# How two DMA rings share the first two loads of a gated SiLU: by partitions instead of by columns

## The chip, the cores and the metric

The kernel runs on one core of a Trainium2 chip. The metric is the device time of one execution in microseconds (us); the kernel before takes 471.64 us, the median of three runs (471.42 to 471.78). Two engines of the core issue the transfers: SyncE (SP in the profile) and ScalarE (ACT). Each has a ring, that is a queue of transfers, on each of the same 16 DMA engines; the profile calls SyncE's ring q1 and ScalarE's q10. A transfer is cut into packets, here one for each partition that it touches, and ends with a small completion mark on each DMA engine.

## The reference

The input has 32 x 512 = 16384 rows of 2048 float32 values. The first half of a row goes through SiLU and is multiplied by the second half:

```python
x1, x2 = x[..., :half_dim], x[..., half_dim:]
silu_x1 = x1 * (1 / (1 + np.exp(-x1)))
return silu_x1 * x2
```

So 134.22 MB are read from HBM and 67.11 MB are written.

## The kernel before

The rows are cut into 16 tiles of 1024 rows. Partition p of a tile holds K = 8 consecutive rows, 64 KB that are contiguous in HBM. Input tiles `xt` and output tiles `ot` are double buffered (`in_pool` and `out_pool`, two buffers each).

The order of the work is written out by hand in the loop over tiles. `load(0)` and `load(1)` are issued first. For each tile `silu` (ScalarE) writes silu of the first halves to `ot`, `mul` (VectorE) multiplies `ot` by the second halves in place, the result is stored by a transfer on ScalarE's ring, and `load(i + 2)` is issued on SyncE's ring. That load reuses the buffer of tile i, so it waits until `mul` of tile i has ended; the store waits for the same. `silu` of tile i waits for the tile's load, and for the store of tile i - 2 that used the same `ot` buffer. A middle tile is one `silu` and one `mul` over all 8 rows; tile 0 is done in four pieces of two rows (`KC_FIRST`), and the last tile in pieces of 2, 2 and 4 rows (`LAST`), each stored by SyncE as soon as it is done. `settle_all_but` makes SyncE see all earlier transfers land before those last ones.

All loads after the first two are one transfer of 8 MB on SyncE's ring. The first two are shared between the rings by `SHARED`: the dictionary holds the row (of the 8 in each partition) at which the tile is cut. Of tile 0, SyncE loads rows 0 to 3 of each partition and ScalarE rows 4 to 7; of tile 1, SyncE loads six rows and ScalarE two. Both transfers of a tile touch all 128 partitions. Line 54 issues every transfer, line 76 is the silu, line 83 the multiplication.

Of the kernel before, what the change touches and what calls it, by code (L numbers as in the profile page):

```python
# [1 line left out]

# [4 lines left out]


@with_exitstack
def kernel(  # L10
    ctx: ExitStack,
    tc: tile.TileContext,
    x: bass.AP,
    out: bass.AP,
):


    nc = tc.nc
    P = nc.NUM_PARTITIONS

    x_flat = x.flatten_outer_dims()
    out_flat = out.flatten_outer_dims()
    num_rows, in_cols = x_flat.shape
    half = in_cols // 2
    dt = x_flat.dtype

    K = 8
    KC_FIRST = 2
    LAST = (2, 2, 4)
    SHARED = {0: K // 2, 1: 3 * K // 4}  # L30
    PLAN = [K] * (num_rows // (P * K))

    in_pool = ctx.enter_context(tc.tile_pool(name="in_pool", bufs=2))
    out_pool = ctx.enter_context(tc.tile_pool(name="out_pool", bufs=2))

    plan = []
    row = 0
    for k in PLAN:
        plan.append((row, k))
        row += P * k  # L40
    assert row == num_rows
    n_tiles = len(plan)

    def view(flat, i):
        row0, k = plan[i]
        return flat[row0:row0 + P * k].rearrange("(p k) d -> p k d", k=k)

    ctx.enter_context(tc.manual_schedule())

    loaded = {}  # L50
    sent = []

    def move(queue, out, in_):
        sent.append(queue.dma_start(out=out, in_=in_).ins)  # L54

    def settle_all_but(n):
        rest = nc.sync.nop(nofuse=True)
        for ins in sent[:-n]:
            tc.add_manual_dep(
                rest.ins,  # L60
                ins.name,
                mybir.DependencyInfo(mybir.DependencyClass.Sync, mybir.DependencyReason.DATA),
                reason="sync sees each earlier transfer land before the last ones",
            )

    def load(i):
        xt = in_pool.tile([P, K, in_cols], dt, name="xt")
        xv = view(x_flat, i)
        cut = SHARED.get(i, K)
        move(nc.sync, xt[:, :cut], xv[:, :cut])  # L70
        if cut < K:
            move(nc.scalar, xt[:, cut:], xv[:, cut:])
        loaded[i] = xt

    def silu(ot, xt, c, ce):
        nc.scalar.activation(  # L76
            out=ot[:, c:ce, :],
            in_=xt[:, c:ce, :half],
            func=mybir.ActivationFunctionType.Silu,
        )  # L80

    def mul(ot, xt, c, ce):
        nc.vector.tensor_mul(  # L83
            out=ot[:, c:ce, :],
            in0=ot[:, c:ce, :],
            in1=xt[:, c:ce, half:],
        )

    load(0)
    load(1)  # L90
    for i in range(n_tiles):
        xt = loaded.pop(i)
        ov = view(out_flat, i)
        ot = out_pool.tile([P, K, half], dt, name="ot")
        if i < n_tiles - 1:
            kc = KC_FIRST if i == 0 else K
            for c in range(0, K, kc):
                silu(ot, xt, c, c + kc)
                mul(ot, xt, c, c + kc)
            move(nc.scalar, ov, ot)  # L100
            if i + 2 < n_tiles:
                load(i + 2)
            continue
        c = 0
        for kc in LAST:
            silu(ot, xt, c, c + kc)
            mul(ot, xt, c, c + kc)
            move(nc.sync, ov[:, c:c + kc], ot[:, c:c + kc])
            c += kc
        settle_all_but(len(LAST))  # L110


# [1 line left out]
_INS = ['x']  # L114
_OUTS = [((32, 512, 1024), 'float32')]


# [23 lines left out]
```

## Time and profile before

| what | value |
|---|---|
| median of three runs | 471.64 us |
| the profiled execution | 471.66 us, span 469.7 us |
| VectorE busy | 139.5 us (30%), 21 instructions |
| ScalarE busy | 114.2 us (24%), 22 instructions |
| one silu, one multiplication of a whole tile | 7.03 us, 8.69 us |
| HBM read and written | 134.22 MB and 67.11 MB, 429 GB/s over the span |
| time of the DMA packets | q1 65.3%, q10 34.2% of 16 engines' span |

A span is the time from the first to the last instruction in the profile. The shares of the rings say how long their packets kept the 16 DMA engines busy. The chain that ended last goes back from the last instruction: at each step to what released it. Times from issue to landing include the time that a transfer waits in its ring behind earlier ones.

### The profile page before, as it was taken

How to read it: one execution, taken by the hardware profiler on the slowest of the kernel's cores; microseconds unless marked ns; L12 is line 12 of the kernel's file. 1: busy time of each engine (PE TensorE's matmuls, PEld its weight loads, DVE VectorE, ACT ScalarE, POOL GpSimd, SP SyncE). 2: the span in 40 equal slices, each digit the busy share in tenths (PEclk: the TensorE clock that was granted, in tenths of full speed). 3: DMA queues.
4: the chain of work that ended last, by engine and by line, in shares of the span. 5: the costliest groups of instructions: out<-in, count | busy, mean ns of one | idle time of the engine just before them, and what ended most of it. 6: DMA issues, size and time to landing. Idle time of an engine off the chain costs nothing.

```text
span 469.7 us, 187 instructions
## 1 busy us (share of the span) xinstructions
DVE 139.5 (30%) x21; ACT 114.2 (24%) x22; POOL 0.2 (0%) x4
## 2 busy tenths in 40 slices
DVE  0070702407034070330704307042070520605142
ACT  1054105032050410504105050050501405014060
POOL 0000000000000000000000000000000000000000
DMA  8999999999999999999999999999999999999998
GB/s 357 424 447 424 402 444 455 441 402 435 413 491 402 410 438 491 402 402 447 474 419 402 447 430 463 402 435 413 491 402 407 441 491 402 402 447 474 419 402 357
DMA packets 5184, 201.33 MB, mean 429 GB/s; under 512 B 576, under 2 KB 576, under 8 KB 576
## 3 DMA queue, kind: packets, MB, share of 16 engines
q1 hardware_dynamic: 2736, 132.12, 65.3%
q10 hardware_dynamic: 2448, 69.21, 34.2%
HBM read 134.22 MB, written 67.11 MB: 429 GB/s over the span
## 4 chain that ended last, share of the span: by engine, by line
DMA 72%; DVE 14%; ACT 12%; ACTq 0%; issue 0%
DMA out_dram<-ot 63%; DVE ot L83 14%; ACT ot L76 12%; DMA xt<-in_x_dram 9%; ACTq L136 0%; ACTq L54 0%
## 5 line engine op out<-in xcount | busy, mean ns | idle before, releaser
L83 DVE TENSOR_TENSOR ot<-ot,xt 128x8192 f32<-128x8192 f32 (+2 forms) x21 | 139.5, 6659 | 321.8 <-ACT ot L76 321.8
L76 ACT ACTIVATE ot<-xt 128x8192 f32<-128x8192 f32 (+2 forms) x21 | 112.9, 5400 | 341.0 <-DMA out_dram<-ot 309.0
L76 ACT ACT_TABLE_LOAD x1 | 1.3, 1283 | 1.6 <-PEq L125 1.6
L125 POOL MEMSET const-bfloat16-1.0<- 128x1 bf16 x1 | 0.1, 101 | 0.0
L125 POOL MEMSET const-uint8-127<- 128x1 uint8 x1 | 0.1, 101 | 0.0
L125 POOL MEMSET const-float32-0.0<- 128x1 f32 x1 | 0.1, 98 | 0.2 <-issue 0.2
L125 POOL MEMSET const-float32-1.0<- 128x1 f32 x1 | 0.1, 98 | 0.0
## 6 DMA issues: line engine op xcount, KB each, us to landing
out_dram<-ot ACTq DMA_DIRECT2D x15, 4096.0 KB, 42.2
xt<-in_x_dram SPq DMA_DIRECT2D x1, 6144.0 KB, 40.9
xt<-in_x_dram ACTq DMA_DIRECT2D x1, 4096.0 KB, 22.1
xt<-in_x_dram SPq DMA_DIRECT2D x1, 4096.0 KB, 21.9
xt<-in_x_dram ACTq DMA_DIRECT2D x1, 2048.0 KB, 41.1
out_dram<-ot SPq DMA_DIRECT2D x2, 1024.0 KB, 7.8
out_dram<-ot SPq DMA_DIRECT2D x1, 2048.0 KB, 7.5
xt<-in_x_dram SPq DMA_DIRECT2D x14, 42.1
```

Of the source, the lines that this page charges most:

```text
L76: nc.scalar.activation(out=ot[:, c:ce, :], in_=xt[:, c:ce, :half], func=mybir.ActivationFunctionType.Silu,)
L83: nc.vector.tensor_mul(out=ot[:, c:ce, :], in0=ot[:, c:ce, :], in1=xt[:, c:ce, half:],)
L125: nc = _bacc.Bacc("TRN2", target_bir_lowering=False, num_devices=1)
```

## The change

`SHARED` is replaced by `SPLIT_LOADS`, which names for tiles 0 and 1 the partitions and the rows that each ring loads. Tile 0: SyncE loads the 64 even partitions, ScalarE the 64 odd ones, each with all 8 rows (64 KB). Tile 1: ScalarE loads the odd partitions in one transfer, SyncE the even ones in four: partitions 2, 6, 10, ... (32 of them), partitions 4, 12, 20, ... (16), and partitions 0, 8, 16, ... (16) twice, once for rows 0 to 3 and once for rows 4 to 7. For each of 16 DMA engines that is 2 + 1 + 1 + 1 packets on SyncE's ring and 4 on ScalarE's, if the partitions are spread evenly over the engines. All other loads and all stores stay as they are.

A tile of one column is added: VectorE sets it to zero, and ScalarE runs silu on it, after the first loads are issued and before tile 0.

```diff
-    SHARED = {0: K // 2, 1: 3 * K // 4}
+    EVERY = slice(None)
+    WHOLE = slice(0, K)
+    SPLIT_LOADS = {
+        0: ([(slice(0, None, 2), WHOLE)], [(slice(1, None, 2), WHOLE)]),
+        1: (
+            [
+                (slice(2, None, 4), WHOLE),
+                (slice(4, None, 8), WHOLE),
+                (slice(0, None, 8), slice(0, K // 2)),
+                (slice(0, None, 8), slice(K // 2, K)),
+            ],
+            [(slice(1, None, 2), WHOLE)],
+        ),
+    }
...
     def load(i):
         xt = in_pool.tile([P, K, in_cols], dt, name="xt")
         xv = view(x_flat, i)
-        cut = SHARED.get(i, K)
-        move(nc.sync, xt[:, :cut], xv[:, :cut])
-        if cut < K:
-            move(nc.scalar, xt[:, cut:], xv[:, cut:])
+        on_sync, on_scalar = SPLIT_LOADS.get(i, ([(EVERY, WHOLE)], []))
+        for ps, ks in on_sync:
+            move(nc.sync, xt[ps, ks], xv[ps, ks])
+        for ps, ks in on_scalar:
+            move(nc.scalar, xt[ps, ks], xv[ps, ks])
         loaded[i] = xt
...
     load(0)
     load(1)
+    prime = ctx.enter_context(tc.tile_pool(name="prime_pool", bufs=1)).tile([P, 1], dt, name="prime")
+    nc.vector.memset(prime, 0.0)
+    nc.scalar.activation(out=prime, in_=prime, func=mybir.ActivationFunctionType.Silu)
     for i in range(n_tiles):
```

## The prediction

> **What bounds the kernel now.** I read the page from the top: part 1 for the engines, part 2 for the DMA, part 6 for the order in which the rings finish; then the chain in order of time for the length of each round, and the timeline for the end.
>
> The page of the kernel before (busy time; the span in 40 slices; queues; bytes):
> ```profile
> DVE 139.5 (30%) x21; ACT 114.2 (24%) x22; POOL 0.2 (0%) x4
> DMA  8999999999999999999999999999999999999998
> ...
> DMA packets 5184, 201.33 MB, mean 429 GB/s; under 512 B 576, under 2 KB 576, under 8 KB 576
> ...
> q1 hardware_dynamic: 2736, 132.12, 65.3%
> q10 hardware_dynamic: 2448, 69.21, 34.2%
> ```
> No engine is busy for a third of the span, but the two rings (q1 is SyncE's, q10 ScalarE's) together take 99.5% of the 16 DMA engines' time. Packets run at 201.33 MB / (0.995 x 469.7 us) = 431 GB/s, 27 for each engine: 64 KB takes 2.42 us, 32 KB 1.21 (so too in the trace's packet records: 2.418 and 1.213). The bytes do not change, so the end moves only by DMA idle time that goes or comes. The 576 tiny packets are completion marks: 36 transfers, one mark on each of 16 engines.
>
> DMA issues of the page (KB, then us from issue to landing):
> ```profile
> out_dram<-ot ACTq DMA_DIRECT2D x15, 4096.0 KB, 42.2
> xt<-in_x_dram SPq DMA_DIRECT2D x1, 6144.0 KB, 40.9
> xt<-in_x_dram ACTq DMA_DIRECT2D x1, 4096.0 KB, 22.1
> xt<-in_x_dram SPq DMA_DIRECT2D x1, 4096.0 KB, 21.9
> xt<-in_x_dram ACTq DMA_DIRECT2D x1, 2048.0 KB, 41.1
> ...
> out_dram<-ot SPq DMA_DIRECT2D x1, 2048.0 KB, 7.5
> xt<-in_x_dram SPq DMA_DIRECT2D x14, 42.1
> ```
> The reader is to see that 6 MB on one ring and 2 MB on the other, issued together, land together (40.9 and 41.1), as do an 8 MB load and a 4 MB store (42.1 and 42.2). So the DMA engines take turns by packet, not by byte: eight packets an engine on each ring finish together whatever their size. In the packet records the marks take a turn of their own as well (data, data, mark, mark).
>
> The chain that ended last (start, us, what):
> ```profile
> 1.16 41.08 DMA xt<-in_x_dram
> ...
> 42.27 7.04 ACT ot L76
> ...
> 58.05 43.21 DMA out_dram<-ot
> ...
> 101.28 7.04 ACT ot L76
> ...
> 117.07 42.21 DMA out_dram<-ot
> ...
> 159.30 7.04 ACT ot L76
> ```
> Two rounds from 101.28 to 159.30 take 58.02 us, 29.01 each. Two rounds from 42.27 to 101.28 take 59.01, with the same packets: 1.0 us was lost once. The timeline puts tile 2's silu at 72.27, so it lies in the first round, and the packet records put it at 41.3 us, where both rings go over to their next transfers at once (tile 2's load, the first store): on all engines that first 64 KB packet takes 3.25 to 3.5 us, 0.84 to 1.1 more than the rest. The very first packet of the run has a like excess, up to 0.89.
>
> The timeline of the end:
> ```profile
> 449.63 7.22 ACT L76 ACTIVATE ot<-xt 128x2048 f32<-128x2048 f32 x3 [21.96 <-DMA out_dram<-ot]
> ...
> 453.89 7.77 SPq L54 DMA_DIRECT2D out_dram<-ot  x3
> ```
> The last tile's silu starts at 449.63; its three stores are issued by 461.33, 11.70 us later, and the last lands 7.5 us after that. The DMA is full up to there because 14's store, and then the first two pieces, are still in the rings; the third piece waits some 1.9 us in its ring (first packet at 463.23 in the records), of which about 1.0 is what any transfer needs from issue to first packet (first load: 0.73 to 1.74). So the end has about 0.9 us in hand: if the last load lands later by more, the DMA goes idle.
>
> **The change part by part.** Sums are against the profiled execution: 471.66 us, span 469.7; the median shown is 471.64, so the two may be used for each other.
>
> Tile 0: 2 x 64 rows of 64 KB in place of 2 x 128 of 32 KB. Each engine gets 4 + 4 packets, not 8 + 8, of the same bytes. Packet overhead is under 5 ns (2 x 1.213 against 2.418), so 15 packets fewer over both tiles give under 0.1 us: nothing. Both halves land near 22 us as now. The first silu now waits for both rings; they land 0.2 us apart today. Hidden by the 14 us that load 2 and store 0 still lie in their rings.
>
> Early activation: the memset costs about 0.1 us (the 128x1 rows of POOL), the activation about 0.2 (what 1.90 us for 2048 columns leaves at the slope of 7.03 for 8192), on a ScalarE that is idle for 19.70 us before tile 0. The table load already runs at 1.65 us. Worth zero; were it not there, and were the load to move behind the wait, 1.28 us would fall on tile 0's compute, which still ends long before its results are needed.
>
> More issues: SyncE issues five transfers at the start in place of two, about 0.4 us each, done by 3 us; the last is needed near 22. Cover: 19 us. Everyone who waits for tile 1 waits for five transfers, not two: today two take 0.18 us (42.09 to 42.27), so up to 0.5, once, on tile 1.
>
> Turns: this decides. For tile 1 SyncE has 2 + 1 + 1 + 1 packets an engine and four marks, ScalarE four packets and one mark. Turn by turn, ScalarE's ring is through when SyncE still has packet, mark, packet, mark (32 KB each). Store 0, issued near 33.7, is ready, so three 32 KB stores slip in before SyncE's last mark. Gain: the rings no longer turn over together, each has the other's packets as cover, and I take the 0.97 us as gone (bounds: 0 and 0.97). Loss: tile 1, and then every load, lands 3 x 1.21 = 3.63 us later in the ring order, since as many stores were served ahead. In the middle this costs nothing, as the DMA is full. Would it decay? A store now spends 42.2 - 29.0 = 13.2 us in its ring before its turn; three turns ahead (3 x 3.63 = 10.9) leave 2.3, less 1.0 from issue to first packet and the 0.5 above: 0.8 us in hand. Tight, but it holds; if not, one turn is lost and the lag is 2.42.
>
> At the end the lag is no longer free. The last silu starts at 449.63 + 3.63 - 0.97 = 452.29, the third piece is issued at 463.99; the DMA, having finished everything else at 463.23 - 0.97 = 462.3, is idle. Landing follows 7.5 - 0.9 = 6.6 us after issue, or 7.5 if a cold ring costs as much as the first packet did (0.87): 470.6 to 471.5, against 468.8 now. That is +1.8 to +2.7. I take +2.2, the middle, as no row shows a cold store: **473.9 us.**
>
> What no row shows is a transfer that touches fewer than 128 partitions. Lower bound: as now, no cost, since all packet sizes (16 to 64 KB) on both rings run at one rate; a gain is excluded, since the DMA engines are already full at that rate. Upper bound by the slowest row: if each of 16 packets an engine paid the 0.95 of the packet at 41.3, +15.2. I take zero, because the rows that it is nearest to (64 KB packets of the same tile) differ only in which partitions they reach.
>
> [...]
>
> **The rivals.** (a) The lag doesn't take hold, for instance because ScalarE's ring needs time to take up the store, while SyncE's packets go on. With one turn of lag the last silu moves by 1.21 - 0.97 = +0.24 and the 0.9 in hand absorbs it: the gap at 41.3 is gone, 470.7 to 471.6. The point from which it decides lies between one turn and two: two give 2.42 - 0.97 - 0.9 = +0.6 or more. For it: the 0.8 us in hand is little. Against: marks take turns, and the store is queued 5 us ahead. (b) The strided halves are slow: up to 471.66 + 15.2 + 2.2 = 489. For it: nothing in this trace has their shape. Against: nothing either but the even rate. (c) The gap stays, since its cause (both rings turning over) is only inferred: with the lag 473.9 + 0.97 = 474.9, without it 471.6, as if nothing were done.
>
> **How the numbers follow.** About 0.2%, 0.94 us, is what can be told from no change. Forecast (lag of two or three turns, gap gone): 0.42, own range 472.2 to 474.4. Lag with the gap kept: 0.08. (b): 0.25. (a): 0.18, of which about half is beyond 0.2%. (c) without lag: 0.07. Faster 0.10, same 0.17, slower 0.73. The range goes from 470.6 (gap gone, nothing lost) to 489 (row bound of (b)); what is left out, worse cases of (b) above all, is under 0.2.
>
> **What would show it.** Tile 1's silu near 45 to 46 us, not 42.27; store 0 landing about 9 us ahead of tile 2, so that silu waits for the load and not for the store; rounds of 29.0 with none of 30; the last silu near 452; a DMA slice below full near 463 to 465. Wrong if tile 0 lands far after 22 us, (b); or if the last silu starts at or before 449.6, (a).

## The result, and the profile after

The changed kernel takes 476.43 us (median of five, 476.11 to 477.92) against 471.64: 1.0106 times as long, 95% interval 1.009 to 1.0123. It is slower, as forecast, but by 4.8 us where 2.3 were forecast. The profiled execution is the slowest of the five, 477.92 us with a span of 475.7; the section on the experiments comes to what sets it apart.

From the page of the changed kernel: DMA busy in 40 slices and GB/s, the two rings, the issues (KB where the page gives it, us to landing).

```profile
DMA  8998999999999999999999999999999999999987
GB/s 353 441 441 265 441 435 435 408 424 452 422 433 430 471 405 446 424 457 405 430 438 441 430 430 463 402 438 438 441 422 433 468 399 438 446 435 413 468 369 298
...
q1 hardware_dynamic: 2672, 130.02, 64.2%
q10 hardware_dynamic: 2320, 71.30, 34.9%
...
out_dram<-ot ACTq DMA_DIRECT2D x15, 4096.0 KB, 33.8
out_dram<-ot SPq DMA_DIRECT2D x2, 1024.0 KB, 5.1
out_dram<-ot SPq DMA_DIRECT2D x1, 2048.0 KB, 6.2
xt<-in_x_dram SPq DMA_DIRECT2D x2, 512.0 KB, 46.0
```

The reader is to see two things. In the fourth slice (36 to 48 us) the DMA moves 265 GB/s where its neighbours move 441; the packet records below have no idle time there, so the packets last longer. (The profile's page counts a packet in the slice in which it starts, hence the 8.) And a store now lands 33.8 us after its issue, not 42.2: stores run ahead of loads.

The timeline of the changed kernel has both, at the start and at the end (start, us, engine, line, operation; in brackets the idle time before it and what ended it):

```profile
23.25 7.31 ACT L90 ACTIVATE ot<-xt 128x2048 f32<-128x2048 f32 x4 [19.70 <-DMA xt<-in_x_dram]
...
51.34 7.03 ACT L90 ACTIVATE ot<-xt 128x8192 f32<-128x8192 f32 x1 [20.78 <-DMA xt<-in_x_dram]
...
80.05 7.03 ACT L90 ACTIVATE ot<-xt 128x8192 f32<-128x8192 f32 x1 [21.68 <-DMA xt<-in_x_dram]
...
456.99 7.22 ACT L90 ACTIVATE ot<-xt 128x2048 f32<-128x2048 f32 x3 [22.03 <-DMA xt<-in_x_dram]
```

Tile 0 is ready at 23.25 (22.63 before): the even and odd partitions bring no slow packets (all but the first of each engine last 2.42 us), and a part of the 0.6 us is SyncE's first issue, which takes 0.57 us in place of 0.38. The first experiment shows that this costs nothing in all. Tile 1 is ready at 51.34, not at 42.27 and not at the 45 to 46 forecast. The last silu starts 7.36 us later than before (449.63), and it now waits for the load alone; before, load and store came in together.

Windows of two microseconds of the changed kernel's end (busy time of VectorE, ScalarE, GpSimd, TensorE clock, DMA share, GB/s):

```profile
465.00:467.00 2.00, 2.00 (x1) 0.00 (x0) 0.00 (x0) 1.00 1.00 422
467.00:469.00 2.00, 1.66 (x1) 0.00 (x0) 0.00 (x0) 1.00 0.15 61
469.00:471.00 2.00, 0.00 (x0) 0.00 (x0) 0.00 (x0) 1.00 0.94 393
```

From 467 to 469 the DMA has almost nothing to move: everything but the last piece is stored, and VectorE is still computing that piece. This idle stretch is the price of loads that land late against stores.

The packet records name the place of the other loss. On one of the 16 DMA engines, in order (start, us, ring, bytes):

```
 31.66  2.418  q10  65536
 34.08  4.673  q1   65536     partitions 4, 12, 20, ...
 38.74  3.034  q10  65536
 41.78  1.973  q1   32768     partitions 0, 8, 16, ..., rows 0 to 3
...
 46.41  1.900  q1   32768     the same, rows 4 to 7
```

The packets of the 16-partition transfers last 4.67 us on this engine (4.5 to 5.0 on all) in place of 2.42, and 1.9 to 2.0 (1.8 to 2.4 on all) in place of 1.21. ScalarE's packets beside them are longer too: 2.6 to 3.1 us for 64 KB in place of 2.42, and up to 1.47 for a store's 32 KB in place of 1.21. From 33 to 52 us the 16 engines each lose 4.9 us on the mean against the usual duration of their packets; in the kernel before it is 1.0, the gap at 41 us.

### The profile page after: what moved, and what is told of

Its sections match the earlier page's. It is cut to its first block, busy times and chain, and to the rows that moved or that the text cites. A ratio compares the mean times of both kernels' runs of the same rounds, so it can differ in the third digit from the quotient of the medians.

```text
span 475.7 us, 197 instructions
## 1 busy us (share of the span) xinstructions
DVE 139.6 (29%) x22; ACT 114.4 (24%) x23; POOL 0.2 (0%) x4
## 4 chain that ended last, share of the span: by engine, by line
DMA 72%; DVE 14%; ACT 11%; SPq 0%; ACTq 0%; issue 0%
DMA xt<-in_x_dram 72%; DVE ot L97 14%; ACT ot L90 11%; SPq L67 0%; ACTq L153 0%; ACTq L90 0%
## 6 DMA issues: line engine op xcount, KB each, us to landing
out_dram<-ot ACTq DMA_DIRECT2D x15, 4096.0 KB, 33.8
xt<-in_x_dram SPq DMA_DIRECT2D x17, 42.1
```

## The experiments

Two theories stood after this. *Partitions*: a transfer is slow by which partitions it touches, whatever the reason, so the packets of 4.7 and 2.0 us stay as long as the sets of 16 stay; against it, *distance*: every eighth partition also means blocks 512 KB apart in HBM. And *lag*: SyncE's ring is some turns behind, which costs about 2 us at the end; against it, the number of transfers or marks. Besides, the prediction had booked the gap at 41 us as gone. All kernels below differ from the changed kernel only as shown, unless said otherwise. The kernel before had medians of 471.46 to 471.56 beside them.

**One transfer of 64 rows.**

```diff
-        1: (
-            [
-                (slice(2, None, 4), WHOLE),
...
+        1: ([(slice(0, None, 2), WHOLE)], [(slice(1, None, 2), WHOLE)]),
```

> SyncE loads the 64 even partitions of tile 1 in one transfer (four packets an engine) in place of four transfers. [...] If the gap at 41 us of the kernel before comes from both rings turning over at once, it is back, about 1 us: 471.7. If it came from the column split, 470.7. If 64-row transfers themselves are slow: above 474.

Measured: 471.82 us, ratio 1.0007 (0.9999 to 1.0016): as the kernel before (eleven of the twelve executions took 471.24 to 471.92, one 474.02). All packets of tiles 0 and 1 but the first last 2.42 us; the gap is there, 1.0 us an engine near 41.4. The last silu, from its timeline:

```profile
449.88 7.22 ACT L82 ACTIVATE ot<-xt 128x2048 f32<-128x2048 f32 x3 [22.01 <-DMA out_dram<-ot]
```

So even and odd partitions, the memset, the early activation and the fewer packets are together worth nothing, and the whole loss lies in how SyncE's share of tile 1 is cut.

**Transfers of 32 rows with the same lag.**

```diff
-                (slice(4, None, 8), WHOLE),
-                (slice(0, None, 8), slice(0, K // 2)),
-                (slice(0, None, 8), slice(K // 2, K)),
+                (slice(0, None, 4), slice(0, K // 2)),
+                (slice(0, None, 4), slice(K // 2, K)),
```

> SyncE's share of tile 1 as three transfers of 32 rows (partitions 2, 6, ...; then 0, 4, ... in two halves of rows): packets and marks keep SyncE as far behind as in the changed kernel, but every transfer has 32 rows four apart. [...] If the loss is in the number of transfers or in the lag itself: 476.

Measured: 473.87 us, ratio 1.0049 (1.0037 to 1.0061). No packet lasts twice as long (the slice from 35 to 47 us has 417 GB/s, where the changed kernel has 265); stores land after 33.7 us as in the changed kernel. Its timeline:

```profile
47.13 7.03 ACT L89 ACTIVATE ot<-xt 128x8192 f32<-128x8192 f32 x1 [16.73 <-DMA xt<-in_x_dram]
...
75.89 7.03 ACT L89 ACTIVATE ot<-xt 128x8192 f32<-128x8192 f32 x1 [21.73 <-DMA xt<-in_x_dram]
...
452.94 7.22 ACT L89 ACTIVATE ot<-xt 128x2048 f32<-128x2048 f32 x3 [22.00 <-DMA xt<-in_x_dram]
```

The last silu is 3.06 us later than with one transfer, the time 2.05 us longer. The remaining 1.0 us is what the end had in hand. So the lag alone costs 2.05 us, and the time is the 473.9 that the prediction gave. The gap is not gone: 0.9 us an engine between 33 and 52 us, now in the packets near 35.5 and 38.2.

**The same, with ScalarE's ring cut alike.**

```diff
-            [(slice(1, None, 2), WHOLE)],
+            [
+                (slice(1, None, 4), WHOLE),
+                (slice(3, None, 4), slice(0, K // 2)),
+                (slice(3, None, 4), slice(K // 2, K)),
+            ],
```

> As the kernel with 32-row transfers on SyncE (473.87), but ScalarE's share of tile 1 is cut in the same way, so both rings take nine turns for tile 1. Lag theory: SyncE is no longer behind, the end is as in the kernel with 64-row transfers: 471.8. If the 2 us come from the number of transfers: 474 or more.

Measured: 471.78 us, ratio 1.0007 (0.9998 to 1.0016), the last silu at 449.95. There are two transfers more than in the kernel of 473.87, and the loss is gone. It is the rings' relative position that costs, not the number of transfers or marks.

**One mark more on SyncE's ring.**

```diff
-            [
-                (slice(2, None, 4), WHOLE),
-                (slice(4, None, 8), WHOLE),
-                (slice(0, None, 8), slice(0, K // 2)),
-                (slice(0, None, 8), slice(K // 2, K)),
-            ],
+            [(slice(2, None, 4), WHOLE), (slice(0, None, 4), WHOLE)],
             [(slice(1, None, 2), WHOLE)],
```

> SyncE's share of tile 1 in two transfers of 32 rows: the same four packets as ScalarE, one completion mark more, so one turn behind. Lag theory: the last silu 1.2 us later than in the kernel with one transfer of 64 rows (449.88), of which 0.9 us is in hand at the end: 472.1. If marks took no turn: 471.8, last silu at 449.9.

Measured: 471.86 us, ratio 1.0008 (0.9999 to 1.0017). The last silu starts at 449.65, not 1.2 us later, and waits for the load alone. A lag of one turn costs nothing that can be measured. It was not lost on the way: tile 1's silu, at 43.72 instead of 42.51, was 1.2 us late, and the last packet of the last load still ends at 449.08 on the last engine, against 448.07 with one transfer. But with one transfer the load's mark stands behind one more store packet (it lands at 449.27), and here it follows the load's last packet at once (449.08). So the first turn of lag is free at the end.

**Other blocks of HBM behind the same partitions.**

```diff
+    FROM = {(1, 4, 8): slice(0, 16), (1, 0, 8): slice(16, 32)}
...
-            move(nc.sync, xt[ps, ks], xv[ps, ks])
+            move(nc.sync, xt[ps, ks], xv[FROM.get((i, ps.start, ps.step), ps), ks])
```

> The 16-row transfers of tile 1 write the same partitions, but read 16 neighbouring blocks of HBM (64 KB apart in place of 512 KB); tile 1 gets wrong rows, all else is the changed kernel. [...] HBM-distance theory: packets of 2.42 and 1.21 us, 472.

Measured: 478.58 us in one run; the engines lose 5.3 us between 33 and 52 us, the packets last 4.6 to 5.2 us and 1.8 to 2.5 us again, where 2.42 and 1.21 are usual. With neighbouring blocks nothing is better: distance in HBM is not the cause.

**Sixteen partitions of one half.**

```diff
-                (slice(4, None, 8), WHOLE),
-                (slice(0, None, 8), slice(0, K // 2)),
-                (slice(0, None, 8), slice(K // 2, K)),
+                (slice(0, 64, 4), WHOLE),
+                (slice(64, None, 4), slice(0, K // 2)),
+                (slice(64, None, 4), slice(K // 2, K)),
```

The 16-row transfers take partitions 0, 4, ... 60 and, in two halves of rows, 64, 68, ... 124: blocks 256 KB apart in HBM.

> [...] HBM-distance theory: 2.42 and 1.21 us, 472.

Measured: 476.68 us in one run; 4.8 us lost between 33 and 52 us; the 64 KB packets last 4.3 to 4.9 us. With blocks 256 KB apart, at which 32 rows ran at full rate, 16 rows are slow again.

**Lower and upper 64 partitions.**

```diff
-        0: ([(slice(0, None, 2), WHOLE)], [(slice(1, None, 2), WHOLE)]),
-        1: (
...
+        0: ([(slice(0, 64), WHOLE)], [(slice(64, None), WHOLE)]),
+        1: ([(slice(0, 64), WHOLE)], [(slice(64, None), WHOLE)]),
```

> Tiles 0 and 1 shared by partitions 0 to 63 and 64 to 127 in place of even and odd, SyncE with four packets as ScalarE. [...] If the loss of the 16-row transfers is only one of few rows: 471.8, as with 64 even and odd ones.

Measured: 510.54 us in one run, 38.7 us more than with even and odd partitions (471.82). Windows of this kernel, and then one of the kernel before, over tiles 0 and 1 (last two columns: DMA share, GB/s):

```profile
22.00:32.00 10.00, 0.00 (x0) 0.00 (x0) 0.00 (x0) 1.00 1.08 229
...
52.00:72.00 20.00, 2.09 (x1) 0.00 (x0) 0.00 (x0) 1.00 0.99 210
```

```profile
22.00:32.00 10.00, 7.42 (x4) 7.31 (x4) 0.00 (x0) 1.00 1.06 459
```

The DMA is busy all the time at half the rate; the 64 KB packets last 4.9 us. Same bytes, same number of rows, same packets and the same turns as with even and odd partitions (471.82): only which partitions differs, and with them the blocks of HBM that a ring reads, which made no difference above. So the choice of partitions is enough for half the rate, with no fewer rows. Whether few rows cost something besides stays open: no run has a set of 16 partitions at the full rate.

**Sixteen neighbouring partitions.**

```diff
-            [
-                (slice(2, None, 4), WHOLE),
...
+            [(slice(p, p + 16), WHOLE) for p in range(0, 64, 16)],
+            [(slice(64, None), WHOLE)],
```

Tile 0 stays by even and odd; of tile 1 ScalarE loads partitions 64 to 127, and SyncE partitions 0 to 63 in four transfers of 16 neighbours.

> [...] If 16 rows cost the same wherever they lie: 4.7 each, 4 x 2.2 = 9 us more: 481.

Measured: 509.82 us in one run, not 481. SyncE's packets last 6.9 to 9.3 us (median 8.6), and ScalarE's between them 5.1 to 5.9. With 16 rows a transfer, packets are slower for neighbouring partitions than for those eight apart (8.6 against 4.7 us); why the two rings share the loss in this way is not shown.

**The slow packets without the lag.** The cut of ScalarE's share above, in the changed kernel.

> The changed kernel with ScalarE's share of tile 1 cut into three transfers of 32 rows, so that both rings take nine turns; SyncE's 16-row transfers stay. [...]

Measured: 476.72 us, ratio 1.0111 (1.0098 to 1.0125). The lag is gone (stores land after 42.2 us), but the engines lose more, 2.3 us at 4 to 33 us and 3.4 at 33 to 52, 5.6 in all. The kernel with 32-row transfers on both rings, which has as many turns on each ring and only the gap, loses about 1.1 there, and takes 4.9 us less. So the slow packets alone cost as much as the whole change in its median. They are not the same as in the changed kernel (the turns fall differently), so the price of the lag in the changed kernel cannot be had by subtraction.

**Without the early activation.**

```diff
-    prime = ctx.enter_context(tc.tile_pool(name="prime_pool", bufs=1)).tile([P, 1], dt, name="prime")
-    nc.vector.memset(prime, 0.0)
-    nc.scalar.activation(out=prime, in_=prime, func=mybir.ActivationFunctionType.Silu)
```

> The changed kernel without the early activation. The table load goes behind the wait for tile 0 or stays ahead of it; at worst tile 0's compute is 1.3 us later, which load 2 and store 0 have in hand: 476.4 as the changed kernel. If the early activation was worth anything: up to 477.7.

Measured: 477.78 us, ratio 1.0132 (1.0118 to 1.0146). Its timeline shows the table load behind the wait for tile 0, and tile 0's silu 1.23 us later for it:

```profile
23.18 1.28 ACT L90 ACT_TABLE_LOAD   x1 [23.18 <-DMA xt<-in_x_dram]
24.48 7.31 ACT L90 ACTIVATE ot<-xt 128x2048 f32<-128x2048 f32 x4
```

The expectation that this is hidden was wrong: the time is 1.35 us longer than that of the changed kernel's median. It is, though, that of the changed kernel's slowest execution. What sets these apart seems to be a turn. If the packet records are strung into 16 chains by their times, then two load packets follow each other at about 68 us, where a store's should have stood between them, on 14 of 16 engines in the profiled execution of the changed kernel, on 15 here, and on all 16 in the kernel with sixteen partitions of one half (476.68). Where one engine does not lose its turn, its part of the load lands a 32 KB packet, 1.21 us, later, and the tile waits for the last engine: silu of tile 2 starts 28.71 us after tile 1's in the changed kernel's profile, and 27.68 in the one with all turns lost. That the four faster executions of the changed kernel lost all 16 turns, and that leaving out the early activation keeps one, is argued from their times, not shown.

**A small store at the start.** In the kernel before, to see whether the gap at 41 us belongs to the first store of the run.

```diff
+    first = ctx.enter_context(tc.tile_pool(name="first_pool", bufs=1)).tile([P, 128], dt, name="first")
+    nc.vector.memset(first, 0.0)
+    move(nc.scalar, view(out_flat, n_tiles - 1)[:, 0, :128], first)
     load(0)
     load(1)
```

> The kernel before, with one small store (512 bytes for each partition, zeros into the last tile's output, which is written again at the end) issued on ScalarE's ring ahead of all loads. If the gap of 1 us at 41 us belongs to the first store of the run, wherever it stands: no gap at 41, and up to 0.9 us less in all if it falls into the start, where the first packets are late anyhow (470.7), or the same time with the gap near 2 us (471.6). If the gap belongs to the turn-over of the rings, or to something that is issued at 33 us: still there, 471.6 or more.

Measured: 476.27 us, ratio 1.0103 (1.0085 to 1.0121). The store's eight packets of 512 bytes an engine take a turn each, so ScalarE's half of tile 0 lands 35.7 us after its issue, not 22.1, and the first multiplications end 10 us late. The run tells about turns, not about the gap: one load packet just ahead of the first whole store is 1.2 us too long (44.8 us), but it also follows some 3 us in which the DMA was idle.

**The same store behind ScalarE's half of tile 0.**

```diff
+    first = ctx.enter_context(tc.tile_pool(name="first_pool", bufs=1)).tile([P, 128], dt, name="first")
+    nc.vector.memset(first, 0.0)
     load(0)
+    move(nc.scalar, view(out_flat, n_tiles - 1)[:, 0, :128], first)
     load(1)
```

> The same small store, but behind ScalarE's half of tile 0 in its ring. If the gap belongs to the first store: it moves to about 21 us, and is gone at 41; time 471.6. Otherwise it stays at 41.

Measured: 483.69 us in one run. Now the 2 MB of tile 1 on ScalarE's ring wait behind the small store, whose 64 KB take eight turns on each engine:

```profile
xt<-in_x_dram SPq DMA_DIRECT2D x1, 6144.0 KB, 36.4
...
xt<-in_x_dram ACTq DMA_DIRECT2D x1, 2048.0 KB, 60.8
```

Tile 1's silu starts at 62.58, the last one at 461.73, 12.1 us later than in the kernel before. As for the gap: it is gone at 41 us, there is none at the small store, and it stands at 58.2 us (0.8 us on the mean), right ahead of the first 32 KB store. A second one, of 1.25 us, stands at 79.5 us, ahead of the second store and behind 8 us in which the DMA was idle. At 36.45 both rings pass from one transfer to the next at the same moment, and there is no gap. So the gap does not come from both rings turning over at once. In the kernel before, in those with one 64-row and with three 32-row transfers, and here, it lies in the one or two load packets just ahead of the first whole store. Why it lies there stays open.

## Why the prediction was wrong

- **Bound by the DMA, end moved only by DMA time lost or won: right.** Every loss was found as long packets or as an idle stretch at the end. The early activation as such cost nothing: 59 ns on VectorE and 203 ns on ScalarE, where 0.1 and 0.2 us were estimated. What it costs to leave it out was put at nothing, and wrongly: 1.35 us, probably through the turn above. By the prediction's own rows a packet's overhead is 8 ns (2 x 1.213 - 2.418), not under 5: 0.12 us for 15 packets, still nothing.
- **Turns: right.** Packets and marks take turns; SyncE falls behind (in the packet records of the changed kernel each engine has a store's 32 KB packet near 43.7, 45.1 and 48.1 us, ahead of SyncE's last mark of tile 1 near 50); stores land 8.3 us ahead of the loads (33.8 and 42.1 us after their issues; about 9 forecast); silu waits for the load and no longer for the store; the DMA is idle at 467 to 469 (463 to 465 forecast, before the slow packets moved it). The kernel that has the lag and no slow packets takes 473.87 us, and 473.9 was the forecast.
- **That sum was made of terms of which three were off and cancelled out.** The gap at 41 us was booked as gone (-0.97): it stayed in every kernel in which it can be told apart (rival (c)). The lag was put at 3.63 us: in the kernel of 473.87 it came to 3.06 at the last silu. A turn is lost there, the possibility that the prediction named, on 6 of 16 engines at 64 us and 10 at the end, but a tile waits for the last engine, and six still have three turns. The 0.57 us are as much as the packets lose less: 0.9 us an engine from 33 to 440 us, against 1.4 with one transfer. And the last store landed 6.2 to 6.3 us after its issue, where the middle taken was 7.05: less than even the lower bound of 6.6, so a cold ring added nothing that shows. That the sum met 473.9 was luck in these terms.
- **The step that failed is "What no row shows is a transfer that touches fewer than 128 partitions [...] I take zero".** It is zero for 64 even or odd partitions and for 32 four apart, and not for the sets of 16: between 33 and 52 us the engines lose 4.9 us in the changed kernel, 3.9 more than in the kernel before and 4.0 more than in the one with 32-row transfers and the same lag. The last silu of the profiled execution starts 4.05 us after the latter's (456.99 and 452.94): the slow packets account for it. Whether the gap is still there among the slow packets can't be told. Against the kernel before the last silu is 7.36 us later, the end gives back 1.3 (7.5 to 6.2 us from issue to landing), and the span is 6.0 us longer. The other four executions took 1.4 to 1.8 us less; that a turn was lost there on all engines is argued from their times.
- **Rival (b) was the right place with a wrong scope.** It was given 0.25 and meant strided halves as such, at up to 15.2 us; its sign, a late tile 0, did not show, as tile 0 has no set of 16. What decides is the set of partitions: the packets of 64 KB lasted 4.7 us for every eighth partition, 2.42 for even or odd ones, 2.42 for every fourth, 4.9 for 0 to 63 and for 64 to 127 (medians), and 6.9 to 9.3 us (median 8.6) for 16 neighbours. Why a set is slow the traces do not show. The prediction put one price on all transfers of fewer than 128 partitions; it should have priced the two 16-row sets alone. Two megabytes at half of the usual rate cost 2 x 2.42 us an engine more: an estimate of 4.8 us from the packets of 2.42 us and the 4.9 of the lower and upper 64 partitions. The slow packets without the lag cost 4.9 (476.72 against 471.78). Added to the 473.9 it gives 478.7: above the slowest execution, 477.92, and 2.3 above the median, so the two costs do not simply add.

No version tried beats the kernel before; those without lag and without slow packets equal it.

## What to carry to other kernels

Which partitions a transfer touches can halve its rate, with their number unchanged (64 KB in 4.9 us in place of 2.42): before cutting a load by partitions, measure the set of partitions of each single piece, down to the smallest. Two rings that take turns by packet make packet counts and marks a schedule: eight packets of 512 bytes delayed 2 MB by 20 us, and a ring that is three turns behind shows no loss until the end, where the last load has no later stores to hide its computation (2.05 us with 32-row transfers). When no row has the shape in question, price each piece of the change by itself, not the whole at once.

## What the runs showed of the hardware

- Sixty-four even, or odd, partitions, and 32 partitions four apart, load at the full rate (2.42 us for 64 KB); by the packet records each of the 16 engines takes 4 or 2 of them. Sixteen partitions eight apart, one packet to an engine, take 4.5 to 5.0 us. The records show the durations, not their reason.
- With one ring loading partitions 0 to 63 and the other 64 to 127, all 64 KB packets of tiles 0 and 1 on both rings took 4.5 to 5.2 us at the start and 4.9 us from then on, for 80 us on end. The engines stayed in step: at 20 moments between 25 and 73 us all 16 were at a packet of the same ring, so at each of these moments only one half of the partitions was written.
- A gap of 0.8 to 1.1 us (mean of the engines) stands just ahead of the first whole store of the run, wherever that is (40.0, 44.6, 44.8, 61.6 us); a small store of 512-byte packets before it neither has it nor takes it away. One run has a second one, behind an idle stretch of the DMA.
- A load can land about 1.2 us (one 32 KB packet) later because one of 16 DMA engines took a store's packet before a load's, as the profiled executions of two kernels show (tile 2's silu 28.71 and 27.68 us after tile 1's). That this also sets executions of one kernel apart is argued.
